# Attention scores of two heads at once on the two row halves of the matrix array, three products for a pair of heads

## The chip, the cores and the metric

The kernel runs on one core of a Trainium2 chip. The metric is the device time of one execution in microseconds (us). The kernel before took 719.02 us (median of 3 runs, 718.4 to 719.49). The engines are TensorE (PE; its weight loads are listed apart as PEld), VectorE (DVE), ScalarE (ACT), GpSimd (POOL) and SyncE (SP), which issues nearly all DMAs.

## What is computed

One decoder block over 512 tokens and 1024 channels, in float32: a retention branch (4 heads) and a forgetting-attention branch (8 heads of 64 channels), merged by sigmoid gates, followed by a SwiGLU feed-forward network. The change lies in the attention branch, which the reference computes for each head and each block of 128 queries as follows (cut):

```python
q_f = rmsnorm(q_f.reshape(B, S, FOX_HEADS, FOX_DH), g_fox_q[l])     # 8 heads of 64
k_f = rmsnorm(k_f.reshape(B, S, FOX_HEADS, FOX_DH), g_fox_k[l])
...
s = jnp.einsum('bhqd,bhkd->bhqk', q_blk, kh).astype(jnp.float32) * scale
s = s + c_blk[..., None] - c[:, :, None, :]          # cumulative forget-gate bias
s = jnp.where(mask[None, None], s, -jnp.inf)
p = jax.nn.softmax(s, axis=-1)
return jnp.einsum('bhqk,bhkd->bhqd', p.astype(vh.dtype), vh)
```

## The kernel before

Large products run in a one-pass float32 format (`float32r`). To keep float32 accuracy each operand is split into a high part h and a low part l = x - h, and a product is made of three: h*h, h*l and l*h (`three`, L165). ACT makes the high part with a cast, DVE the low part with a subtraction.

The work goes in stages: the input projections, the retention branch, the attention branch, the output projections and merge (`feat`, L529, with `w_y`), the output product `w_o`, and the feed-forward network. While a branch with long chains of small steps runs, PE is given other work between its pieces: the object `fill` (L554) holds generators of projection products, and `fill(us)` emits about so many microseconds of them. In the attention branch the fill is the tail of the value projection and the gate products `gates(0)` and `gates(1)` (products named acc<-xh,wh, acc<-xl,wh and acc<-xh,wl in the trace). PE's instructions in this branch are pinned to the order in which the code emits them (L553 to L644). Instructions emitted after L644 are not pinned: the scheduler may set the output projections of `w_y` (acc<-orh, acc<-orl, acc<-ofh, acc<-ofl) earlier, where it expects PE to wait.

The attention branch takes the 8 heads as 4 pairs a of heads e = 0, 1. The channels of a pair fill 128 rows, 64 for each head.

- `fox_prep(a, part)` (L458) turns k (part 0) or q (part 1) of a pair with four PE transposes into a PSUM bank of the tag `tp` and splits it. For each head it makes tiles of all 128 rows. `tk[e]` holds the high part of k twice, once on either half (two ACT passes, L467 and L468); `kl[e]` holds the low part on the head's own rows (DVE, L469) and zeros on the others, which POOL set once (L623). `tq[e]` holds the high part of q on the head's own rows (ACT, L477) and its low part on the other half (DVE, L478).
- `fox_scores(a, e, i)` (L481) makes the scores of one head and one query block i against keys 0 to n = 128(i+1): two products of 128 rows into a `sc` bank. The first (sc<-tk,tq) gives qh*kh + ql*kh, the second (sc<-kl,tq) gives qh*kl. The moving width is m = max(n, 256): 512, 384, 256 and 256 for i = 3, 2, 1, 0. POOL adds the causal mask to the bias (L491), DVE adds the bias and takes the row minimum (L499), ACT takes the exponential (L501), DVE the reciprocal and the scaling (L502, L503).
- `fox_turn(a, e, i)` (L506) turns the finished probabilities with i+1 PE transposes (tp<-ctab,pr) into a `tp` bank, and DVE (i = 3, L516) or ACT (L518) copies them to `pT`.
- `fox_values(a)` (L520) multiplies them with v for both heads (sc<-pT,vf; each head on one half of the array's columns) into a `sc` bank, which ACT and DVE split (L171, L172).

There are two `tp` and two `sc` banks. The loop at L629 walks the 32 head-blocks in the order i = 3, 2, 1, 0 within a head: at each step the scores of one head-block, the turn of the head-block three steps earlier (LAG = 3), after eight of them the values of a pair, and a piece of fill (SF, L133). The preparation of the next pair stands at steps 3 and 5 of 8.

In the retention branch, earlier in the kernel, four sets of products already use half of the array's rows: `ret_scores` (tp<-rT, L358) and the second part of `ret_values` (sc<-sn,rT, L385) have 64 rows, with even heads on the lower and odd heads on the upper half.

Of the kernel before, what the change touches and what calls it, by code (L numbers as in the profile page):

```python
# [21 lines left out]
NK = D // P  # L22
RH, RDK, RDV = 4, 64, 128
FH, FD = 8, 64
# [29 lines left out]
def block_kernel(ctx: ExitStack, tc, x, xT, c_early, c_tab, c_late, w_qf, w_tok, w_a, w_y, w_o, w_gu, w_dn, w_dh, out):  # L54
    nc = tc.nc
    PS = bass.MemoryType.PSUM
    tt, ts, stt = nc.vector.tensor_tensor, nc.vector.tensor_scalar, nc.vector.scalar_tensor_tensor
    act = nc.scalar.activation
# [12 lines left out]
    def mm(o, **kw):  # L71
        in_order(nc.tensor.matmul(o, **kw))  # L72

    def turn(o, src):
        in_order(nc.tensor.transpose(out=o, in_=src, identity=ident))  # L75

    def f32(ap):
        return ap.bitcast(F32)
# [7 lines left out]
    sm = ctx.enter_context(tc.tile_pool(name="sm", bufs=2, side="right"))  # L86
# [4 lines left out]
    def bank(tag):  # L91
        return ps.tile([P, 512], F32, name=tag, tag=tag, bufs={"acc": 4, "sc": 2, "tp": 2}[tag])
# [5 lines left out]
    gq = cst.tile([P, 1], F32, name="gq")  # L98
# [104 lines left out]
    for k in range(NK):  # L203
        h, l = first_units[k // 2]
# [111 lines left out]
    gp = nc.gpsimd  # L316
# [138 lines left out]
    ra, rb = slice(0, FD), slice(FD, P)  # L455
    fox = {}

    def fox_prep(a, part):  # L458

        if part == 0:  # L460
            tk = [fwk.tile([P, S], F32R, name="tk", tag=f"tk{e}", bufs=TB) for e in range(2)]
            kl = kls[a % TB]
            pk = bank("tp")
            for t in range(NT):
                turn(pk[:, t * P:(t + 1) * P], kf[:, t, a * P:(a + 1) * P])
            for e, (r, o) in enumerate(((ra, rb), (rb, ra))):
                act(out=tk[e][r], in_=pk[r], func=AF.Copy, scale=gk[r])  # L467
                act(out=tk[e][o], in_=pk[r], func=AF.Copy, scale=gk[r])  # L468
                stt(out=kl[e][r], in0=pk[r], scalar=gk[r], in1=f32(tk[e])[r], op0=ALU.mult, op1=ALU.subtract)  # L469
            fox["k", a] = tk, kl  # L470
        else:
            tq = [fwk.tile([P, S], F32R, name="tq", tag=f"tq{e}", bufs=TB) for e in range(2)]
            pq = bank("tp")
            for t in range(NT):
                turn(pq[:, t * P:(t + 1) * P], qf[:, t, a * P:(a + 1) * P])
            for e, (r, o) in enumerate(((ra, rb), (rb, ra))):
                act(out=tq[e][r], in_=pq[r], func=AF.Copy, scale=gq[r])  # L477
                stt(out=tq[e][o], in0=pq[r], scalar=gq[r], in1=f32(tq[e])[r], op0=ALU.mult, op1=ALU.subtract)  # L478
            fox["q", a] = tq

    def fox_scores(a, e, i):  # L481

        tq, (tk, kl) = fox["q", a], fox["k", a]
        if i == NT - 1:
            fox["cb"] = fox_bias(2 * a + e)
            fox["pT", a, e] = fwk.tile([P, 3 * 384 + S], F32, name="pT", tag="pT", bufs=PT)
        cb = fox["cb"]
        n = (i + 1) * P
        m = max(n, 256)
        qs = slice(i * P, n)  # L490
        gp.tensor_tensor(out=cb[:, qs], in0=cb[:, qs], in1=mask, op=ALU.add)  # L491
# [3 lines left out]
        pr = fwk.tile([P, S], F32, name="pr", tag="pr", bufs=PR)  # L495
        nm = sm.tile([P, 1], F32, name="nm", tag="nm", bufs=4)
        rs = sm.tile([P, 1], F32, name="rs", tag="rs", bufs=4)
        ri = sm.tile([P, 1], F32, name="ri", tag="ri", bufs=4)
        nc.vector.tensor_tensor_reduce(out=pr[:, :n], in0=cb[:, :n], in1=sc[:, :n], scale=-1.0, scalar=3e38,  # L499
                                       op0=ALU.add, op1=ALU.min, accum_out=nm)  # L500
        fox["last"] = act(out=pr[:, :n], in_=pr[:, :n], func=AF.Exp, scale=-1.0, bias=nm, accum_out=rs)  # L501
        nc.vector.reciprocal(out=ri, in_=rs)  # L502
        ts(out=pr[:, :n], in0=pr[:, :n], scalar1=ri, scalar2=None, op0=ALU.mult)  # L503
        fox["pr", a, e, i] = pr

    def fox_turn(a, e, i):  # L506

        pr, pT = fox["pr", a, e, i], fox["pT", a, e]
        pt = bank("tp")
        for j in range(i + 1):  # L510
            turn(pt[:, j * P:(j + 1) * P], pr[:, j * P:(j + 1) * P])
        row = pT[:, i * P:(i + 1) * P]
        dst = bass.AP(tensor=row.tensor, offset=row.offset, ap=[row.ap[0], [384, i + 1], [1, P]])
        src = pt[:, :(i + 1) * P].rearrange("p (j q) -> p j q", j=i + 1)
        if i == 3:
            nc.vector.tensor_copy(out=dst, in_=src)  # L516
        else:
            nc.scalar.copy(out=dst, in_=src)  # L518
# [98 lines left out]
    ofl = ofp.tile([P, 4, S], F32R, name="ofl")  # L617

    fill(CF[2])
    kls = [[fwk.tile([P, S], F32R, name="kl", tag=f"kl{b}{e}", bufs=1) for e in range(2)] for b in range(TB)]  # L620
    for pair in kls:
        for e, o in enumerate((rb, ra)):
            gp.memset(f32(pair[e])[o], 0.0)  # L623
    fox_prep(0, 1)
    fill(CF[3])
    fox_prep(0, 0)
    fill(PF)
    chain = [(a, e, i) for a in range(4) for e in range(2) for i in reversed(range(NT))]
    for s in range(len(chain) + LAG + 2):  # L629
        if s < len(chain):  # L630
            fox_scores(*chain[s])
            if s % 8 in PREP and s // 8 < 3:
                fill(SF[0] / 2)
                fox_prep(s // 8 + 1, PREP.index(s % 8))
        if LAG <= s < len(chain) + LAG:
            fox_turn(*chain[s - LAG])
        v = s - LAG - 1
        if v >= 0 and v % 8 == 7:
            if v == 7:
                fill.until(2)  # L640
            fox_values(v // 8)
        fill(SF[chain[min(s, len(chain) - 1)][2]])
    fill.until(1)
    pinned[0] = False  # L644
    fwk.release()
# [417 lines left out]
```

## Time and profile before

| | before |
|---|---|
| median of 3 runs (range) | 719.02 us (718.4 to 719.49) |
| profiled execution: time | 720.08 us |
| profiled execution: span of the profile | 718.3 us |
| clock granted to TensorE | 1.00 |
| PE busy | 708.7 us, 99% of the span |
| PEld busy | 623.2 us, 87% |
| DVE busy | 508.9 us, 71% |
| ACT busy | 343.8 us, 48% |
| POOL busy | 70.7 us, 10% |

A matmul row of the timeline gives its start and a modelled duration. Matmuls overlap, so the pace is read from the distance between starts: a product of width 512 lasts 0.39 us by its row, but the next starts about 0.23 us later. For the same reason PE's busy share is high even where it waits a little; a wait shows as a distance between starts that is larger than the pace. One float32 product (not float32r) appears as two records, so four products are x8. The median of the shown runs lies 1.06 us below the profiled execution.

### The profile page before, as it was taken

The numbers are of one execution on the slowest core, as the hardware profiler recorded it, in microseconds if no ns is written. First come the engines' busy times: TensorE is split into PE (matmuls) and PEld (weight loads), VectorE is DVE, ScalarE is ACT, GpSimd is POOL, SyncE is SP. The second block draws the span as 40 slices with busy tenths as digits, with TensorE's granted clock in tenths as the row PEclk, the third lists the DMA queues.
The fourth block names the chain that finished last, engine by engine and source line by source line (L and its number), as shares of the span: only waits on it lengthen the run. The fifth ranks groups of instructions, "written<-read, shape, count | busy, mean of one in ns | idle before, by whom it ended". The sixth has DMA issues, their size and how long they took to land.

```text
span 718.3 us, 10861 instructions
## 1 busy us (share of the span) xinstructions
PE 708.7 (99%) x4307; PEld 623.2 (87%) x4307; DVE 508.9 (71%) x844; ACT 343.8 (48%) x532; POOL 70.7 (10%) x90
## 2 busy tenths in 40 slices
PE   8999999999999999999999999999999999999997
PEld 6888998888776688888888999999999997888997
DVE  6343667756878664536968889898989998834694
ACT  4532334446666733324653755565565545422241
POOL 0163502212221100000120000000000000000000
PEclk9999999999999999999999999999999999999999
DMA  8632222234212033237403323332233124631111
GB/s 278 253 118 89 74 76 74 75 107 149 99 45 74 29 103 103 88 91 256 180 1 117 112 69 114 118 118 70 109 118 118 59 67 131 205 127 59 57 63 60
DMA packets 19908, 76.34 MB, mean 106 GB/s; under 512 B 2312, under 2 KB 2952, under 8 KB 16656
## 3 DMA queue, kind: packets, MB, share of 16 engines
q1 hardware_dynamic: 19712, 75.62, 31.0%
q8 instruction: 34, 0.56, 0.3%
q14 instruction: 18, 0.15, 0.1%
q10 hardware_dynamic: 144, 0.02, 0.0%
HBM read 73.52 MB, written 2.11 MB: 105 GB/s over the span
## 4 chain that ended last, share of the span: by engine, by line
PE 92%; DVE 3%; ACT 2%; DMA 2%; issue 1%; POOL 0%; SPq 0%; DVEq 0%; ACTq 0%
PE acc L72 60%; PE sc L72 26%; PE tp L72 5%; PE tp L75 2%; DMA t<-in_w_dn_dram 1%; DVE pr L499 1%; DMA raw<-in_w_tok_dram 1%; POOL cb L491 0%; ACT ah L862 0%; DVE pr L503 0%; ACT xfh L692 0%; DVE tq L478 0%; ACT pr L501 0%; DVE kl L469 0%; ACT tk L468 0%
## 5 line engine op out<-in xcount | busy, mean ns | idle before, releaser
L152 ACT CAST wh<-raw 128x1024 fp32r<-128x1024 f32 (+1 forms) x52 | 54.5, 1050 | 122.5 <-PE acc L72 97.4
L153 DVE TENSOR_TENSOR wl<-raw,wh 128x1024 fp32r<-128x1024 f32 (+1 forms) x52 | 66.6, 1282 | 47.6 <-ACT wh L152 47.4
L72 PE MATMUL sc<-xfh,cl 128*128 128x256 f32 x288 | 83.3, 289 | 0.0
L72 PE MATMUL sc<-xfh,ch 128*128 128x256 f32 x288 | 81.6, 283 | 1.2 <-DVE u L944 1.0
L72 PE MATMUL sc<-xfl,ch 128*128 128x256 f32 x288 | 81.4, 283 | 0.0
L72 PE MATMUL acc<-wh,xh 128*128 128x512 f32 (+2 forms) x192 | 69.7, 363 | 0.1
L740 DVE TENSOR_TENSOR cl<-t,ch 128x1024 fp32r<-128x1024 f32 x48 | 58.6, 1222 | 13.7 <-ACT ch L740 13.6
L72 PE MATMUL acc<-wh,xl 128*128 128x512 f32 (+2 forms) x192 | 68.2, 355 | 0.0
L72 PE MATMUL acc<-wl,xh 128*128 128x512 f32 (+2 forms) x192 | 68.0, 354 | 0.0
L72 PE MATMUL acc<-xfh,ah 128*128 128x256 f32 (+1 forms) x216 | 63.9, 296 | 0.0
L72 PE MATMUL acc<-xfh,al 128*128 128x256 f32 (+1 forms) x216 | 63.7, 295 | 0.0
L72 PE MATMUL acc<-xfl,ah 128*128 128x256 f32 (+1 forms) x216 | 63.7, 295 | 0.0
L740 ACT CAST ch<-t 128x1024 fp32r<-128x1024 f32 x48 | 50.5, 1053 | 12.8 <-PE tp L72 8.0
L72 PEld LDWEIGHTS sc<-xfh,ch 128*128 128x128 f32 x288 | 55.1, 191 | 1.6 <-issue 1.2
L72 PEld LDWEIGHTS sc<-xfh,cl 128*128 128x128 f32 x288 | 55.0, 191 | 0.9 <-DVE cl L740 0.2
L72 PEld LDWEIGHTS sc<-xfl,ch 128*128 128x128 f32 x288 | 55.1, 191 | 0.0
L72 PE MATMUL acc<-xh,wh 128*128 128x512 f32 x128 | 51.8, 405 | 0.0
L72 PE MATMUL acc<-xh,wl 128*128 128x512 f32 x128 | 50.1, 391 | 0.0
L72 PE MATMUL acc<-xl,wh 128*128 128x512 f32 x128 | 49.9, 390 | 0.0
L740 DVE TENSOR_TENSOR al<-raw,ah 128x1536 fp32r<-128x1536 f32 x24 | 42.2, 1757 | 6.9 <-ACT ah L740 6.9
L72 PEld LDWEIGHTS acc<-xfh,al 128*128 128x128 f32 x216 | 41.3, 191 | 1.0
L72 PEld LDWEIGHTS acc<-xfl,ah 128*128 128x128 f32 x216 | 41.3, 191 | 0.9
(298 smaller groups left out, 1795.3 us busy)
## 6 DMA issues: line engine op xcount, KB each, us to landing
raw<-in_w_gu_dram SPq DMA_DIRECT2D x21, 1024.0 KB, 4.8
raw<-in_w_tok_dram SPq DMA_DIRECT2D x16, 512.0 KB, 3.6
raw<-in_w_a_dram SPq DMA_DIRECT2D x16, 512.0 KB, 3.6
t<-in_w_dn_dram SPq DMA_DIRECT2D x14, 512.0 KB, 3.7
raw<-in_w_y_dram SPq DMA_DIRECT2D x8, 512.0 KB, 3.7
raw<-in_w_o_dram SPq DMA_DIRECT2D x8, 512.0 KB, 3.7
raw<-in_w_dh_dram SPq DMA_DIRECT2D x4, 1024.0 KB, 6.4
xf<-in_xT_dram SPq DMA_DIRECT2D x8, 256.0 KB, 5.0
```

The costliest lines, as they stand in the source:

```text
L72: in_order(nc.tensor.matmul(o, **kw))
L75: in_order(nc.tensor.transpose(out=o, in_=src, identity=ident))
L152: nc.scalar.copy(out=h[:, :width], in_=raw[:, :width])
L153: tt(out=l[:, :width], in0=raw[:, :width], in1=f32(h)[:, :width], op=ALU.subtract)
L499: nc.vector.tensor_tensor_reduce(out=pr[:, :n], in0=cb[:, :n], in1=sc[:, :n], scale=-1.0, scalar=3e38, op0=ALU.add, op1=ALU.min, accum_out=nm)
L740: split_to.last = nc.scalar.copy(out=h, in_=src), tt(out=l, in0=src, in1=f32(h), op=ALU.subtract)
```

## The change

- `fox_prep` makes, for a pair, one high tile (`kh` or `qh`, one ACT pass over 128 rows) and one low tile (`kl` or `ql`, one DVE pass). The doubled and zero-padded halves are gone, and so are POOL's four memsets.
- `fox_scores(a, i)` makes both heads' scores of a query block: three products for each head (qh*kh, ql*kh, qh*kl), each on the 64 rows of its head, the heads alternating, each head into its own `sc` bank. The widths m stay. The softmax steps follow for e = 0, then e = 1.
- `fox_turn(a, i)` turns both heads' probabilities.
- The loop walks 16 pair-blocks. At step p it emits the values of the previous pair (at p % 4 == 2, followed by fill), then the turn of the pair-block two steps earlier, then the scores of block p, then fill with other amounts. The preparation of the next pair stands at p % 4 = 1 (k) and 2 (q).
- Buffers: `pT` 2 instead of 3, `pr` 6 instead of 4, bias rows `cb` 5 instead of 3. The fill ahead of the first scores is 4.0 instead of 5.9 us.

```diff
-    RAW, WB, SG, PT, PR, TB, CBUF = 2, 3, 8, 3, 4, 2, 3
-    PREP = [3, 5]
-    RF, CF, PF, SF, LAG = (5.32, 4.64, 5.6, 4.6, 11.2), (3.0, 2.0, 2.26, 4.0), 5.9, (0.83, 1.03, 1.77, 1.6), 3
+    RAW, WB, SG, PT, PR, TB, CBUF = 2, 3, 8, 2, 6, 2, 5
+    RF, CF, PF, SF = (5.32, 4.64, 5.6, 4.6, 11.2), (3.0, 2.0, 2.26, 4.0), 4.0, (3.6, 2.9, 1.0, 2.4)
...
-            for e, (r, o) in enumerate(((ra, rb), (rb, ra))):
-                act(out=tk[e][r], in_=pk[r], func=AF.Copy, scale=gk[r])
-                act(out=tk[e][o], in_=pk[r], func=AF.Copy, scale=gk[r])
-                stt(out=kl[e][r], in0=pk[r], scalar=gk[r], in1=f32(tk[e])[r], op0=ALU.mult, op1=ALU.subtract)
...
+        h = fwk.tile([P, S], F32R, name=nm + "h", tag=nm + "h", bufs=TB)
+        l = fwk.tile([P, S], F32R, name=nm + "l", tag=nm + "l", bufs=TB)
+        pk = bank("tp")
+        for t in range(NT):
+            turn(pk[:, t * P:(t + 1) * P], src[:, t, a * P:(a + 1) * P])
+        act(out=h, in_=pk, func=AF.Copy, scale=gain)
+        stt(out=l, in0=pk, scalar=gain, in1=f32(h), op0=ALU.mult, op1=ALU.subtract)
...
-        sc = bank("sc")
-        mm(sc[:, :m], lhsT=tq[e][:, qs], rhs=tk[e][:, :m], start=True, stop=False)
-        mm(sc[:, :m], lhsT=tq[e][:, qs], rhs=kl[e][:, :m], start=False, stop=True)
+        sc = [bank("sc") for _ in range(2)]
+        for g, (x, y) in enumerate(((qh, kh), (ql, kh), (qh, kl))):
+            for e, r in enumerate(heads):
+                mm(sc[e][:, :m], lhsT=x[r, qs], rhs=y[r, :m], start=g == 0, stop=g == 2)
...
-    chain = [(a, e, i) for a in range(4) for e in range(2) for i in reversed(range(NT))]
-    for s in range(len(chain) + LAG + 2):
-        if s < len(chain):
-            fox_scores(*chain[s])
-            if s % 8 in PREP and s // 8 < 3:
-                fill(SF[0] / 2)
-                fox_prep(s // 8 + 1, PREP.index(s % 8))
-        if LAG <= s < len(chain) + LAG:
-            fox_turn(*chain[s - LAG])
...
+    chain = [(a, i) for a in range(4) for i in reversed(range(NT))]
+    for p in range(len(chain) + 3):
+        if p >= 6 and p % 4 == 2:
+            if p == 6:
+                fill.until(2)
+            fox_values(p // 4 - 1)
+            fill(SF[2])
+        if 2 <= p < len(chain) + 2:
+            fox_turn(*chain[p - 2])
+        if p < len(chain):
+            fox_scores(*chain[p])
+            if p // 4 < 3 and p % 4 in (1, 2):
+                fill(SF[p % 4] / 2)
+                fox_prep(p // 4 + 1, p % 4 - 1)
+                fill(SF[p % 4] / 2)
+                continue
+        fill(SF[p % 4])
```

PE's first 755 rows and everything from the first `w_y` products behind the branch on are the same in both programs. In the middle of the branch, on PE before, the end of a head: scores (sc), a turn of probabilities (tp<-ctab,pr) and gate products (acc) take turns one head at a time.

```order
L72 MATMUL sc<-tk,tq 128x256
L72 MATMUL sc<-kl,tq 128x256
L75 MATMUL tp<-ctab,pr 128x128
L72 MATMUL acc<-xh,wh 128x512
L72 MATMUL acc<-xl,wh 128x512
L72 MATMUL acc<-xh,wl 128x512
L72 MATMUL sc<-tk,tq 128x256
L72 MATMUL sc<-kl,tq 128x256
```

The same place on PE in the changed kernel, here with what each row waits for; tp<-ctab,qf is the transposition of the next pair's q.

```order
L75 MATMUL tp<-ctab,qf 128x128 [waits DVE_49]
L75 MATMUL tp<-ctab,qf 128x128 x3
L72 MATMUL acc<-xh,wh 128x512
L72 MATMUL acc<-xl,wh 128x512
L72 MATMUL acc<-xh,wl 128x512
L75 MATMUL tp<-ctab,pr 128x128 [waits Activation_49]
L75 MATMUL tp<-ctab,pr 128x128 x2
L75 MATMUL tp<-ctab,pr 128x128 [waits Activation_49]
L75 MATMUL tp<-ctab,pr 128x128 x2
L72 MATMUL sc<-kh,qh 128x256 [waits DVE_49] x2
L72 MATMUL sc<-kh,ql 128x256 x2
L72 MATMUL sc<-kl,qh 128x256 x2
```

The scores of a pair-block now stand as one block of six products on half rows between full-row work, and the turns of both heads follow one another; the second head's turn waits for ACT. Towards the end of the branch, on PE before, the last head's scores stand with single `w_y` products between them.

```order
L72 MATMUL sc<-tk,tq 128x384
L72 MATMUL sc<-kl,tq 128x384
L75 MATMUL tp<-ctab,pr 128x128 x2
L72 MATMUL sc<-tk,tq 128x256
L72 MATMUL sc<-kl,tq 128x256
L75 MATMUL tp<-ctab,pr 128x128
L72 MATMUL acc<-ofh,wh 128x512
L72 MATMUL sc<-tk,tq 128x256
L72 MATMUL sc<-kl,tq 128x256
```

And in the changed kernel, the last pair's block i = 1:

```order
L75 MATMUL tp<-ctab,pr 128x128 x8
L72 MATMUL sc<-kh,qh 128x256
L72 MATMUL acc<-orh,wh 128x512
L72 MATMUL acc<-orl,wh 128x512
L72 MATMUL acc<-orh,wl 128x512
L72 MATMUL acc<-orh,wh 128x512
L72 MATMUL acc<-orl,wh 128x512
L72 MATMUL sc<-kh,qh 128x256
L72 MATMUL sc<-kh,ql 128x256 x2
L72 MATMUL sc<-kl,qh 128x256 x2
```

Here the scheduler has put full-row products between the first head's and the second head's first product, so that the block is entered twice. This happens three times, at the last pair's blocks i = 2, 1 and 0.

More of the change, by code (lines that the diff above doesn't have):

```diff
@@ L490, in fox_scores @@
         qs = slice(i * P, n)
-        gp.tensor_tensor(out=cb[:, qs], in0=cb[:, qs], in1=mask, op=ALU.add)
-        sc = bank("sc")
-        mm(sc[:, :m], lhsT=tq[e][:, qs], rhs=tk[e][:, :m], start=True, stop=False)
-        mm(sc[:, :m], lhsT=tq[e][:, qs], rhs=kl[e][:, :m], start=False, stop=True)
[L495 to L518, printed above, removed]
+        sc = [bank("sc") for _ in range(2)]
@@ new lines, in fox_turn @@
+    def fox_turn(a, i):
+        for e in range(2):
+            pr, pT = fox["pr", a, e, i], fox["pT", a, e]
+            pt = bank("tp")
+            for j in range(i + 1):
+                turn(pt[:, j * P:(j + 1) * P], pr[:, j * P:(j + 1) * P])
+            row = pT[:, i * P:(i + 1) * P]
+            dst = bass.AP(tensor=row.tensor, offset=row.offset, ap=[row.ap[0], [384, i + 1], [1, P]])
+            src = pt[:, :(i + 1) * P].rearrange("p (j q) -> p j q", j=i + 1)
+            if i == 3 and e == 0:
+                nc.vector.tensor_copy(out=dst, in_=src)
+            else:
+                nc.scalar.copy(out=dst, in_=src)
@@ L619, in block_kernel @@
     fill(CF[2])
[L620 to L623, printed above, removed]
     fox_prep(0, 1)
```

49 lines of the change are left out of this document (22 added, 27 removed).

## The prediction

> **What bounds the kernel now.** I read the page first, for the engine that carries the span and for the chain of work that ended last.
>
> ```profile
> span 718.3 us, 10861 instructions
> PE 708.7 (99%) x4307; PEld 623.2 (87%) x4307; DVE 508.9 (71%) x844; ACT 343.8 (48%) x532; POOL 70.7 (10%) x90
> PE 92%; DVE 3%; ACT 2%; DMA 2%; issue 1%; POOL 0%; SPq 0%; DVEq 0%; ACTq 0%
> ```
>
> PE is busy for 99% of the span and makes 92% of the chain. The attention branch gives PE gate products between its steps, so PE is the bound there too: what the change is worth is PE's time for the rows that differ, and PE's waits among them. The table of stretches for the part of PE's order that differs (84.0 us) shows the other engines:
>
> ```profile
> core 0: us, PE busy (x) PEld busy (x) DVE busy (x) ACT busy (x) POOL busy (x), PEclk, DMA share, GB/s
> 166.10:250.10 84.00, 82.42 (x440) 63.10 (x439) 62.87 (x171) 57.11 (x130) 17.22 (x30) 1.00 0.22 71
> ```
>
> DVE is busy for 75% and ACT for 68%, so neither bounds the stretch as a whole; but PE waits for single steps of theirs. The granted clock is 1.00 and DMA stands at 0.22, so I keep both out of the sum. From PE's timeline I take the pace of the scores, as distances between starts:
>
> ```profile
> 168.79 0.39 PE L72 MATMUL sc<-tk,tq 128*128 128x512 f32 x1
> 169.01 0.39 PE L72 MATMUL sc<-kl,tq 128*128 128x512 f32 x1
> 169.24 0.39 PE L72 MATMUL acc<-xh,wh 128*128 128x512 f32 x1
> ...
> 171.28 0.33 PE L72 MATMUL sc<-tk,tq 128*128 128x384 f32 x1
> 171.45 0.34 PE L72 MATMUL sc<-kl,tq 128*128 128x384 f32 x1
> 171.63 0.40 PE L72 MATMUL acc<-xh,wh 128*128 128x512 f32 x1
> ...
> 173.01 0.28 PE L72 MATMUL sc<-tk,tq 128*128 128x256 f32 x1
> 173.12 0.28 PE L72 MATMUL sc<-kl,tq 128*128 128x256 f32 x1
> 173.24 0.40 PE L72 MATMUL acc<-xh,wh 128*128 128x512 f32 x1
> ```
>
> Two products take 0.45 us at width 512, 0.35 at 384 and 0.23 at 256: 0.225, 0.175 and 0.115 each, with nothing lost on entering or leaving, since all these rows use the whole array. PE's waits in the stretch show as larger distances:
>
> ```profile
> 206.93 0.40 PE L72 MATMUL acc<-orh,wh 128*128 128x512 f32 x1
> 207.57 0.50 PE L72 MATMUL sc<-tk,tq 128*128 128x512 f32 x1 [0.24 <-DVE nm L499]
> ...
> 224.51 0.40 PE L72 MATMUL acc<-orh,wh 128*128 128x512 f32 x1
> 225.48 0.33 PE L75 MATMUL tp<-ctab,pr 128*128 128x128 f32 x1 [0.57 <-ACT pT L518]
> ...
> 231.85 0.40 PE L72 MATMUL acc<-orh,wl 128*128 128x512 f32 x1
> 232.42 0.63 PE L75 MATMUL tp<-ctab,pr 128*128 128x128 f32 x4 [0.17 <-DVE pr L503]
> ...
> 240.81 0.40 PE L72 MATMUL acc<-ofh,wh 128*128 128x512 f32 x1
> 241.56 0.52 PE L75 MATMUL tp<-ctab,pr 128*128 128x128 f32 x3 [0.34 <-DVE pr L503]
> ```
>
> Against the pace of 0.23 the four lose 0.41, 0.74, 0.34 and 0.52, together 2.0 us. The smaller ones, each under 0.4, I estimate at 1.4 more: 3.4 us of waits.
>
> **Part one, the products.** Before, a query block of a pair costs two heads times two products, four widths in line. After, it is three for each head, and if the two heads' products run at the same time, three widths. The pair's four blocks have one product each at 0.225 and 0.175 and two at 0.115, 0.63 us for one product of each block; four pairs save 4 x 0.63 = 2.5 us. Whether halves run at the same time is seen in the retention branch, where products of 64 rows stand beside full-row ones (float32, each x8 is four products of width 128):
>
> ```profile
> 95.56 1.05 PE L72 MATMUL sc<-vr,sT 128*128 128x128 f32 x8
> 96.54 0.72 PE L72 MATMUL sc<-sn,rT 64*128 64x128 f32 x8
> 97.09 0.71 PE L72 MATMUL tp<-rT 64*128 64x128 f32 x8
> ...
> 134.66 1.05 PE L72 MATMUL sc<-vr,sT 128*128 128x128 f32 x8
> 135.64 0.72 PE L72 MATMUL sc<-sn,rT 64*128 64x128 f32 x8
> 136.29 0.50 PE L72 MATMUL acc<-wh,xh 128*128 128x512 f32 x1
> 136.63 0.40 PE L72 MATMUL acc<-wl,xh 128*128 128x512 f32 x1
> ```
>
> Eight full-row records take 0.98 us, eight half-row ones 0.55: on the two halves they do overlap. No row shows it for float32r, so the bounds are three widths (-2.5 us) and six, one after the other: 4 x 0.63 x 2 = +5.0 us. I take the first, since the nearest row is the same array at the same row split.
>
> A rule of the Trainium skill gives less here: "TensorE: Matmul & The Clock Gate", Part 3, "Measured speedup vs the span model", reports 3.07 for four row tiles, 77% of the full factor. As an estimate, 1.53 instead of 2 would make the three widths cost 3.9 and leave 0.2 us of the 2.5, so that the forecast would lie 2.3 us higher. The retention rows speak for nearly the full factor once entering and leaving are taken out.
>
> **Part two, entering and leaving.** The same rows give the price. Leaving: half rows before half rows take 0.55 (96.54 to 97.09), the same work before full rows 0.65 (135.64 to 136.29), so the change of mode costs 0.10 at the border. Then 0.98 for eight full-row records holds one such border and leaves 0.88, 0.11 each. In the 0.55 four steps of two at once, 0.44, leave 0.11: the first weights after the border are not loaded ahead. The same shows behind the block, where the next gate product starts 0.34 later (136.29 to 136.63) instead of 0.23. In and out therefore cost 0.10 + 0.11 + 0.10 + 0.11 = 0.42, and I use 0.4 for rounding. Sixteen pair-blocks give 16 x 0.4 = +6.4 us. The lower bound is 0.2 a block, +3.2, if the weights of float32r can be loaded ahead; the upper 0.5, +8.0. I take 6.4, as the row that follows here is the same kind of gate product. Before, none of this was paid for the scores.
>
> In the changed order the last pair's blocks i = 2, 1 and 0 have `w_y` products between the two heads' first products. Each then enters and leaves twice (0.4) and has one width that runs alone (0.175, 0.115 and 0.115): 1.6 us if nothing covers it. The filler stands there because the second `sc` bank is expected late, so part falls into waits that would be there anyway: +0.8, between 0 and 1.6.
>
> The Trainium skill, "TensorE: Matmul & The Clock Gate", Part 3, "The mechanism", lets a weight load overlap a running product only where the row groups differ; by that rule the alternating heads would be better off than full rows. The case's weight loads on the whole array speak against it:
>
> ```profile
> 168.56 0.19 PEld L72 LDWEIGHTS sc<-tk,tq 128*128 128x128 f32 x1
> 168.79 0.19 PEld L72 LDWEIGHTS sc<-kl,tq 128*128 128x128 f32 x1
> ```
>
> The load for kl,tq starts with the product tk,tq and is hidden beneath it. By the rule the 64 old products would each pay 0.19 us, and the new ones nothing: 12 us of gain that the pace of 0.225 leaves no room for.
>
> **Part three, ACT and DVE.** The groups of ACT and DVE in the branch (count, busy us, mean ns, idle before):
>
> ```profile
> L468 ACT ACTIVATE tk<-tp,ce 64x512 fp32r<-64x512 f32 x8 | 5.5, 683 | 0.1
> L477 ACT ACTIVATE tq<-tp,gq 64x512 fp32r<-64x512 f32 x8 | 5.4, 681 | 1.7 <-DVE tq L478 1.2 <-PE tp L75 0.2
> L467 ACT ACTIVATE tk<-tp,ce 64x512 fp32r<-64x512 f32 x8 | 5.4, 679 | 2.5 <-DVE kl L469 2.4
> L478 DVE SCALAR_TENSOR_TENSOR tq<-tp,gq,tq 64x512 fp32r<-64x512 f32 x8 | 6.0, 750 | 1.0 <-ACT tq L477 0.8
> L469 DVE SCALAR_TENSOR_TENSOR kl<-tp,ce,tk 64x512 fp32r<-64x512 f32 x8 | 6.0, 750 | 6.1 <-ACT tk L468 6.1
> L499 DVE CUSTOM_DVE_ANT_0 pr<-cb,sc 128x256 f32<-128x256 f32 x8 | 3.3, 414 | 0.4 <-POOL cb L491 0.4
> L501 ACT ACTIVATION_READ_ACCUMULATOR pr<-pr,nm 128x1 f32 x32 | 6.0, 187 | 0.0
> L501 ACT ACTIVATE pr<-pr,nm 128x256 f32<-128x256 f32 x8 | 4.1, 511 | 5.7 <-DVE nm L499 5.3 <-DVE ri L502 0.4
> L518 ACT COPY pT<-tp 128x384 f32<-128x384 f32 x8 | 3.8, 470 | 1.3 <-PE tp L75 1.2
> ```
>
> ACT makes 24 passes of 0.68 us and will make 8, with the same 512 elements in a row: 16 x 0.68 = 11 us less. DVE makes 16 passes and will make 8: 8 x 0.75 = 6 us less. None of it is on PE, so it counts only through waits. The softmax steps, turns and values keep their number and widths. POOL's memsets and the order of SP's bias loads lie beside PE's work; in the open they would cost a bias load's landing, for which I add nothing as the first four are issued together ahead of the scores.
>
> New waits come from two places. The turn of a pair needs two `tp` banks; beside the preparation of q, the second head's turn waits for ACT. From the end of a block's scores (width 256) a row minimum (0.41), two exponentials with the reading of their sums (0.51 + 0.19 each), the cast of q (0.68) and the copy of the first head's turn (0.47) stand in line, 3.0 us; PE has six gate products (6 x 0.23) and seven transposes (0.11 each, the float32 record of part two) until it needs that bank, 2.2 us. That is 0.8 us at two places in the middle, 1.6 in all. And each block needs both `sc` banks, so the values' bank must be split before the scores of the next block. In the old kernel scores need one bank at a time. On the other side, the lighter ACT and DVE should take away most of the 2.0 us quoted above. I put the waits of the new kernel at 2.7 us, between 0 and 6: -0.7 against 3.4.
>
> **The sum.** -2.5 + 6.4 + 0.8 - 0.7 = +4.0 us. The profiled execution took 720.08, so its like would take 724.1; the median of the runs shown lies 1.06 lower, at 719.02, and the forecast is 723.0. A measurement of this kernel can tell about 0.2% from no change, 1.4 us.
>
> **The rivals.**
> - *Slower by more: float32r products do not overlap on the two halves.* Then part one is +5.0 instead of -2.5 and all else stays: +11.5, 730.5. For it: no row shows float32r on half rows. Against it: the float32 rows overlap. Chance 0.10.
> - *About the same: PE's waits go.* Two heads at once put more filler between a score and its turn, and ACT has 11 us less to do; if all 3.4 us of waits go and the split blocks cost nothing: -2.5 + 6.4 - 3.4 = +0.5, 719.5. For it, the waits quoted are for ACT's copies and DVE's scaling, whose queues get shorter; against it, the tail keeps its chain of softmax steps. Chance 0.20.
> - *Faster: the borders are half hidden.* If float32r weights are loaded ahead across the border, a block pays 0.2 instead of 0.4; with the waits gone too: -2.5 + 3.2 - 3.4 = -2.7, 716.3. With all waits gone, a block has to cost less than 0.28 for a gain over 1.4 us. For it: PE's loads run ahead elsewhere. Against it: 0.34 instead of 0.23 is a float32r product. Chance 0.17.
>
> **How the numbers follow.** The forecast, slower by 1.5 to 8 us, has 0.53; its own range is 720.5 to 727. The slower side is 0.53 + 0.10 and a little of the second case, 0.65; the second case leaves 0.18 for the same, and faster keeps 0.17. From 716.5 to 728 all is held but the first rival and the lower half of the third.
>
> **What would show it.** Right: the scores of a block as pairs of rows with starts almost together; a gap of about 0.2 us ahead of each block, and the first product behind it at 0.34; the stretch of 84.0 us growing to 88. Wrong in part one: six equal distances within a block. Wrong in part two: a first product behind a block at 0.23. Wrong in part three: waits over 6 us, or none, between the first scores and the last values; the row of the second head's turn beside tp<-ctab,qf shows it first.

## The result

The changed kernel takes 723.03 us (median of 6 runs, 721.98 to 724.3). The kernel before, run beside it, takes 718.77 (6 runs, 718.35 to 719.49). The ratio is 1.0060, 95% interval 1.0048 to 1.0072: 4.3 us slower, where 4.0 was forecast. That the total agrees proves little; the terms behind it are gone through below, and two of them were off.

The page of the changed kernel, its span, its engines and its chain:

```profile
span 720.9 us, 10889 instructions
PE 710.1 (99%) x4339; PEld 619.4 (86%) x4339; DVE 501.0 (70%) x832; ACT 334.7 (46%) x520; POOL 65.1 (9%) x86
PE 92%; DMA 2%; DVE 2%; ACT 1%; issue 1%; SPq 0%; DVEq 0%; ACTq 0%
```

ACT has lost 9 us of work and DVE 8 (11 and 6 were worked out). Most of that difference has a cause that the description of the change leaves out: at i = 3 DVE now copies only the first head's turn (`if i == 3 and e == 0`), and ACT the second's, so four copies of 0.6 to 0.7 us have moved from DVE to ACT. PE still makes 92% of the chain, with 32 products more than before. The stretch in which PE's order differs, from the same gate product on one side to the same row on the other (83.84 us before, by the starts of rows):

```profile
core 0: us, PE busy (x) PEld busy (x) DVE busy (x) ACT busy (x) POOL busy (x), PEclk, DMA share, GB/s
165.50:252.20 86.70, 85.03 (x471) 60.49 (x470) 57.99 (x164) 49.87 (x120) 12.48 (x28) 1.00 0.19 61
```

It is 2.9 us longer. PE's timeline of the first block of scores, to be held against the rows of 168.79 to 169.24 in the prediction:

```profile
165.52 0.39 PE L72 MATMUL acc<-xh,wl 128*128 128x512 f32 x1
165.84 0.50 PE L72 MATMUL sc<-kh,qh 64*128 64x512 f32 x2
166.17 0.40 PE L72 MATMUL sc<-kh,ql 64*128 64x512 f32 x2
166.41 0.40 PE L72 MATMUL sc<-kl,qh 64*128 64x512 f32 x2
166.73 0.50 PE L72 MATMUL acc<-xh,wh 128*128 128x512 f32 x1
167.07 0.40 PE L72 MATMUL acc<-xl,wh 128*128 128x512 f32 x1
167.31 0.39 PE L72 MATMUL acc<-xh,wl 128*128 128x512 f32 x1
```

Each x2 is one product of either head. The steps are 0.32, 0.33, 0.24, 0.32, 0.34, 0.24. The five steps from 165.52 to 167.07 take 1.55, where five at the pace of 0.227 would take 1.14. Four of them hold the border: 0.09 before the block, 0.10 behind its first products, 0.09 after the block and 0.11 behind the first gate product, 0.39 in all.

PE's waits are now at the turn of the second head beside the preparation of q, the place that the prediction named:

```profile
178.53 0.49 PE L75 MATMUL tp<-ctab,pr 128*128 128x128 f32 x3
180.05 0.55 PE L75 MATMUL tp<-ctab,pr 128*128 128x128 f32 x3 [1.04 <-ACT pT L511]
...
200.62 0.49 PE L75 MATMUL tp<-ctab,pr 128*128 128x128 f32 x3
201.68 0.55 PE L75 MATMUL tp<-ctab,pr 128*128 128x128 f32 x3 [0.57 <-ACT pT L511]
```

Three transposes take about 0.32; the distances are 1.52 and 1.06, so 1.2 and 0.7 us are waited. The block that is entered twice, i = 2 of the last pair:

```profile
229.72 0.39 PE L72 MATMUL acc<-orh,wh 128*128 128x512 f32 x1
230.17 0.44 PE L72 MATMUL sc<-kh,qh 64*128 64x384 f32 x1
230.54 0.50 PE L72 MATMUL acc<-orl,wh 128*128 128x512 f32 x1
...
231.20 0.44 PE L72 MATMUL sc<-kh,qh 64*128 64x384 f32 x1
231.21 0.61 PE L72 MATMUL sc<-kh,ql 64*128 64x384 f32 x2
```

The first head's first product stands alone between gate products and pays the border for itself.

**Two differences lie outside the stretch.** One belongs to the profiled execution of before. Its first products, then the same of the changed kernel:

```profile
5.76 0.76 PE L72 MATMUL sc<-wh,xh 128*128 128x512 f32 x1 [0.87 <-DVE wh L195]
...
7.09 1.05 PE L72 MATMUL tp<-wh,xh 128*128 128x512 f32 x2
7.95 1.05 PE L72 MATMUL sc<-wh,xl 128*128 128x512 f32 x2
```

```profile
5.68 0.47 PE L72 MATMUL sc<-wh,xh 128*128 128x512 f32 x1 [0.90 <-DVE wh L194]
...
6.41 0.62 PE L72 MATMUL tp<-wh,xh 128*128 128x512 f32 x2
6.86 0.62 PE L72 MATMUL sc<-wh,xl 128*128 128x512 f32 x2
```

Two products take 0.86 us in the one (7.09 to 7.95) and 0.45 in the other (6.41 to 6.86), steps of 0.43 against 0.23: until 9.6 us the profiled execution of before ran at half pace. The last gate product that both programs share ahead of the stretch starts at 166.52 there and at 165.52 in the changed kernel. That 1.0 us is the start of this execution, not the change. The profiled spans differ by 2.6 us and the medians by 4.3; this start accounts for 1.0 of the 1.7 between them, and another 0.4 lies outside the span of the profile, where the changed kernel's execution has 2.2 us and the other 1.8.

The other lies at 596 us, in the feed-forward network, 345 us behind the last changed instruction. PE's waits there before, and in the changed kernel:

```profile
PE sc L72 <- ACT d L808: 1.5, 1, 1.5
```

```profile
PE sc L72 <- ACT d L799: 2.4, 1, 2.4
```

PE waits for a copy on ACT, and ACT's queue stands behind a cast that waits for a weight transfer. That cast, before and after:

```profile
594.77 1.05 ACT L862 CAST ah<-t 128x1024 fp32r<-128x1024 f32 x1 [1.71 <-DMA t<-in_w_dn_dram]
```

```profile
597.32 1.05 ACT L853 CAST ah<-t 128x1024 fp32r<-128x1024 f32 x1 [2.57 <-DMA t<-in_w_dn_dram]
```

The same transfer costs 0.9 us more. This was not foreseen; experiments 9 to 11 show why.

### The profile page after: what moved, and what is told of

Read it like the earlier page. It is cut to its first block, busy times and chain, and to the rows that moved or that the text cites. A ratio compares the mean times of both kernels' runs of the same rounds, so it can differ in the third digit from the quotient of the medians.

```text
span 720.9 us, 10889 instructions
## 1 busy us (share of the span) xinstructions
PE 710.1 (99%) x4339; PEld 619.4 (86%) x4339; DVE 501.0 (70%) x832; ACT 334.7 (46%) x520; POOL 65.1 (9%) x86
## 4 chain that ended last, share of the span: by engine, by line
PE 92%; DMA 2%; DVE 2%; ACT 1%; issue 1%; SPq 0%; DVEq 0%; ACTq 0%
PE acc L72 61%; PE sc L72 25%; PE tp L72 4%; PE tp L75 2%; DMA raw<-in_w_tok_dram 1%; DMA t<-in_w_dn_dram 1%; DVE cl L731 0%; ACT xfh L683 0%; DVE al L854 0%; DVE ot L922 0%; ACT qf L439 0%; ACT ah L853 0%; DVE t L740 0%; DVE pf L896 0%; DVE pr L491 0%
```

## The experiments

Theory: both heads run at the same time, which gives the 2.5 us; each entry into half rows costs 0.39 us, which takes 6.2 us for sixteen and 7.4 for nineteen; the rest is waits. Rivals: the halves do not really overlap; or the loop over pairs with its waits makes the time, whatever the rows. Each ratio is against runs of the kernel before that were taken beside the experiment; a gap is the distance between two starts, and half pace means steps of 0.43 us between products of width 512 instead of 0.23. Where the text says "in the branch", it compares the time in the traces between two products that all the kernels share, one ahead of the attention branch and one behind it (at 138.23 and 259.65 us before).

**1. Head after head.**

```
-        for g, (x, y) in enumerate(((qh, kh), (ql, kh), (qh, kl))):
-            for e, r in enumerate(heads):
+        for e, r in enumerate(heads):
+            for g, (x, y) in enumerate(((qh, kh), (ql, kh), (qh, kl))):
```

> The changed kernel with one head's three products before the other's, so that only the last of the first head and the first of the second can run together. Theory (the halves overlap): five widths in line instead of three, 2 x 0.63 us for each of four pairs, +5.0; its program enters half rows 17 times instead of 19, about -0.8; so 727 us against 723.0. Rival (float32r products on the two halves do not overlap anyway): 723, no difference, and equal distances between the six starts of a block.

725.0 us (5 runs), ratio 1.0085 (1.0072 to 1.0098). The experiment did not do what it was for. In the program all three products of the first head now stand ahead of the second's, but in fourteen of the sixteen blocks they start in pairs on the chip as before:

```profile
165.43 0.50 PE L72 MATMUL sc<-kh,qh 64*128 64x512 f32 x2
165.76 0.40 PE L72 MATMUL sc<-kh,ql 64*128 64x512 f32 x2
166.00 0.40 PE L72 MATMUL sc<-kl,qh 64*128 64x512 f32 x2
```

Only in the last pair's blocks i = 2 and i = 1 does the second head come later, and there the heads run in line:

```profile
230.29 0.44 PE L72 MATMUL sc<-kh,qh 64*128 64x384 f32 x1
230.57 0.33 PE L72 MATMUL sc<-kh,ql 64*128 64x384 f32 x1
230.75 0.33 PE L72 MATMUL sc<-kl,qh 64*128 64x384 f32 x1
230.90 0.44 PE L72 MATMUL sc<-kh,qh 64*128 64x384 f32 x1
```

So the order of the heads is of no account where the second one has not to wait. Of the 2 us on top of the changed kernel 0.6 lie in the branch; the rest has another source (below, at 596 us). To force all products into line took another edit.

**2. Both heads on the same half.** The second head's scores are left out and the first's are made twice, so that all six products use the same 64 rows.

```
-                mm(sc[e][:, :m], lhsT=x[r, qs], rhs=y[r, :m], start=g == 0, stop=g == 2)
+                mm(sc[e][:, :m], lhsT=x[heads[0], qs], rhs=y[heads[0], :m], start=g == 0, stop=g == 2)
```

> The changed kernel with the second head of a pair computed from the first head's rows of q and k, so that both heads' products use the same half of the array's rows (the second head's scores are left out, the first's are computed twice). Number, shape and order of all instructions stay. Theory (the two halves run at the same time, which saves three widths a block; the loss is the border of 0.39 us a block and the waits): six widths in line instead of three, 4 x 0.63 x 3 = 7.5 us more than the changed kernel's 723.0, so 730.5. Rival (the halves overlap only in the records, and the time of the changed kernel is that of six products in line): no difference, 723.

730.95 us (4 runs), ratio 1.0161 (1.0148 to 1.0174).

```profile
166.18 0.73 PE L72 MATMUL sc<-kh,qh 64*128 64x512 f32 x2
166.75 0.63 PE L72 MATMUL sc<-kh,ql 64*128 64x512 f32 x2
167.22 0.62 PE L72 MATMUL sc<-kl,qh 64*128 64x512 f32 x2
167.77 0.50 PE L72 MATMUL acc<-xh,wh 128*128 128x512 f32 x1
```

Each pair now takes 0.47 to 0.57 instead of 0.24 to 0.33, and the whole costs 7.9 us by the medians, 7.3 by the ratios, against 7.5 worked out. Not all of that is scores: in the profiled execution (731.9) 6.6 us lie in the branch, with 0.3 less of waits, and 1.9 behind it, from 596 us on. The rows of the scores by themselves grow from 11.8 to 19.1 us, 7.3. The overlap is real and nearly full; the first rival of the prediction is out.

**3. Twelve entries more.** Behind the first pair of products a piece of fill is put, and its time taken off the next fill: 31 entries instead of 19, the same work.

```
                 mm(sc[e][:, :m], lhsT=x[r, qs], rhs=y[r, :m], start=g == 0, stop=g == 2)
+            if g == 0:
+                fill.step()
+                fill.debt -= S * MM3
```

> The changed kernel with three gate products (taken from the fill that follows) set between the first two and the last four products of each block, as long as there is fill: half rows are entered 31 times instead of 19, with the same work. Theory (0.4 us for each entering and leaving): 12 x 0.4 = +4.8, 727.8 us. Rival (the time of the change comes from the loop over pairs and its waits, not from the borders): within 0.5 us of 723.0.

730.76 us (5 runs, 729.45 to 732.92), ratio 1.0159 (1.0140 to 1.0178): 7.7 us for 4.8 expected. Of the rest, waits in the stretch grew from 1.9 to 3.0 us and the gap at 596 us from 2.75 to 3.34; behind it thirteen products ran at half pace (2.9 us) in the profiled execution, which took 732.38. The two executions with a granted clock of 1.000 took 729.45 and 729.65: 4.7 + 1.1 + 0.6 = 6.4 on 723.0. In the branch it takes 5.9 us more; less the 1.1 of waits that is 4.8, or 0.40 an entry. The price per entry holds, and the rival (within 0.5 us) is out; the experiment moved more than it meant to.

**4. Five entries less.** The last two query blocks of a pair, both of width 256, are made in one bank, back to back: 14 entries.

```
-        sc = [bank("sc") for _ in range(2)]
...
+        if i:
+            fox["sc"] = [bank("sc") for _ in range(2)]
+            for b in (1, 0) if i == 1 else (i,):
+                w = slice(256, 512) if b == 0 else slice(0, m)
...
+        sc = [b[:, 256:512] if i == 0 else b for b in fox["sc"]]
```

> The changed kernel with the scores of a pair's blocks i = 1 and i = 0 made together, both in one bank, so that half rows are entered 14 times instead of 19. Theory: -5 x 0.4 and about -0.2 for widths that no longer run alone: 720.8 us. Rival (waits for the banks make the time): 723 or more, since a bank is held longer.

723.34 us (5 runs), ratio 1.0055 (1.0041 to 1.0068): no gain; by its time, the rival's. The scores' rows do shrink, from 11.8 to 10.8 us. But waits in the stretch are 2.5 us, and the gap at 596 us is 3.32. In the branch the kernel does gain 1.6 us, or 2.1 with waits as before, 0.4 for each of five entries; the part behind the branch takes 0.7 of it back in the profiled execution.

**5. Pairs with full rows.** The loop over pairs and its buffers (bias rows 4 instead of 5) with the old preparation for each head and the old two full-row products.

```
...
+        for e in range(2):
+            mm(sc[e][:, :m], lhsT=tq[e][:, qs], rhs=tk[e][:, :m], start=True, stop=False)
+            mm(sc[e][:, :m], lhsT=tq[e][:, qs], rhs=kl[e][:, :m], start=False, stop=True)
...
```

> The loop over pairs, its fill and its buffers as in the changed kernel (bias rows 4 instead of 5, for room), but q and k prepared as before and two products on full rows for each head. Theory: +2.5 for the fourth width, -16 x 0.4 for the borders and -1.6 for the three blocks entered twice, +0 to +1 for the heavier preparation: 717.5 to 718.5 us, slightly under the kernel before. Rival (the loop over pairs makes the time): 723 or more.

722.11 us (5 runs), ratio 1.0036 (1.0023 to 1.0049): slower than before without any half rows. My theory missed it.

```profile
178.93 0.49 PE L75 MATMUL tp<-ctab,pr 128*128 128x128 f32 x3
181.37 0.55 PE L75 MATMUL tp<-ctab,pr 128*128 128x128 f32 x3 [1.95 <-ACT pT L512]
...
183.12 0.63 PE L72 MATMUL acc<-xh,wh 128*128 128x512 f32 x1
183.55 0.63 PE L72 MATMUL acc<-xl,wh 128*128 128x512 f32 x1
183.97 0.63 PE L72 MATMUL acc<-xh,wl 128*128 128x512 f32 x1
```

The wait for the second head's bank is 2.1 us here, and behind it eight gate products step by 0.43 instead of 0.23, 1.6 us. So the rival has a part of the truth: the loop over pairs is slow by itself, in the place where the preparation of q meets the two turns. The next two runs take that place away.

**6 and 7. The preparation one step earlier**, in the changed kernel and in the kernel of experiment 5.

```
-            if p // 4 < 3 and p % 4 in (1, 2):
+            if p // 4 < 3 and p % 4 in (0, 1):
...
-                fox_prep(p // 4 + 1, p % 4 - 1)
+                fox_prep(p // 4 + 1, p % 4)
```

> The changed kernel with the next pair's k prepared after a pair's first scores and q after its second, instead of after the second and the third. Number and shape of all instructions stay. Theory (PE waits for the second head's tp bank because ACT has the cast of q to do between the exponentials and the copy of the first head's turn; 1.2 + 0.7 us in the changed kernel): these two waits go, 723.0 - 1.9 = 721.1. Rival (ACT is late there whatever it does before, or the wait moves to the step that now has the cast beside it): no difference, 723.0.

724.2 us (6 runs, 722.07 to 725.35), ratio 1.0060 (1.0044 to 1.0076): no gain. Yet both waits are gone. The turn that waited 1.2 us now runs through, and from the first score to the last value the kernel takes 78.95 us (one gate product less lies in it) instead of 81.05, the 1.9 us that were expected:

```profile
178.92 0.82 PE L75 MATMUL tp<-ctab,pr 128*128 128x128 f32 x6
```

They are given back at 596 us:

```profile
595.88 0.39 PE L72 MATMUL sc<-hl,al 128*128 128x512 f32 x1
599.25 1.22 PE L72 MATMUL sc<-hl,ah 128*128 128x512 f32 x2 [2.98 <-ACT d L799]
600.27 0.63 PE L72 MATMUL sc<-hl,al 128*128 128x512 f32 x1
600.70 1.05 PE L72 MATMUL acc<-hl,ah 128*128 128x512 f32 x2
```

A gap of 3.37 us, and then twelve products at 0.43 instead of 0.23; with the steps on either side of them that is 2.7 us. By the time, the rival's "no difference" was right; but the wait has not moved to a step beside the cast, as it had it, and the one at 596 us is another (experiments 9 to 11).

> The kernel with pairs but the old full-row products (722.1 us, with waits of 5.1 us in the stretch and products at half pace for 3.4 us behind the longest of them), with k and q of the next pair prepared one step earlier as well. Theory (the pair's loop is slow only through the waits beside the preparation of k and q and the slow pace behind them; half rows cost the rest): 1.2 + 2.1 + 0.7 us of waits and 1.7 us of slow pace go, 722.1 - 5.7 = 716.4, faster than both kernels. Rival (two heads at once need two tp banks at once, and the wait only moves): 721 to 723.

717.88 us (11 runs, 716.13 to 718.84), ratio 0.9977 (0.9968 to 0.9986), where 716.4 was expected: 1.6 us faster than before, the only kernel here that beats both. The full-row loop over pairs keeps 2.6 us of waits, of which this is the largest, but no half pace, and the gap at 596 us is 1.73.

```profile
PE tp L75 <- DVE pT L510: 1.0, 1, 1.0
```

**8. No block entered twice.** A block's first product also waits for DVE's last reading of the `sc` banks (`fox["free"]`), so that both are free: 16 entries.

```
+                first = nc.tensor.matmul(sc[e][:, :m], lhsT=x[r, qs], rhs=y[r, :m], start=g == 0, stop=g == 2)
...
+                if g == e == 0 and "free" in fox:
+                    tc.add_manual_dep(first.ins, fox["free"].ins.name, mybir.DependencyInfo(mybir.DependencyClass.Sync, mybir.DependencyReason.DATA), reason="both banks")
...
```

> The changed kernel with the first product of a block's scores waiting until both sc banks are free, so that no other product stands between the heads' first products and half rows are entered 16 times instead of 19. Theory (each of the three double entries costs a border of 0.39 us and a width of 0.12 to 0.18 alone, and hides no wait): 723.0 - 1.6 = 721.4. Rival (the filler between them covers a wait for the second bank that now shows): 723.0.

724.39 us (6 runs, 721.69 to 727.2), ratio 1.0070 (1.0048 to 1.0091). Inconclusive by its time, since the profiled execution again has a gap of 3.24 us at 596 and thirteen products at half pace; the two executions with a granted clock of 1.000 took 721.69 and 722.95. By its rows the scores shrink by 1.0 us and a wait of 0.6 appears ahead of the values at 233.9; in the branch the kernel gains 1.0. So 0.6 of the 1.6 us of the double entries was covered.

**9 to 11. Code against weights.** The gap at 596 us was 1.7 to 1.9 in the kernels with full rows (before, 5, 7) and 2.75 to 3.4 in all seven with half rows. The page lists two queues of instruction loads; the larger, q8, has 34 packets, 0.56 MB, 16 KB each. PE makes 4339 products and as many weight loads, so if these are PE's, one packet is 128 products of its code. The queue's packet nearest to the place, in windows of half a microsecond: before, it ran at 600.0 us; after, at 595.0, in the middle of the transfer that ACT waits for:

```profile
q8 instruction: 1, 0.02, 11.7%
```

In all seven half-row kernels (after, 1 to 4, 6, 8) it ran 2.3 to 3.8 us ahead of the late cast; in the three with full rows it came 5 us behind it. The change adds 32 products, a quarter of a packet's worth and 7.3 us at the pace of 0.227, and so moves every later load of PE's code ahead: against the late cast by 7.5 us, from 5.2 behind it before to 2.3 ahead of it after. The awaited transfer itself takes 4.6 to 5.2 us from issue to landing in the seven kernels, and 3.6 to 3.7 in the three. To test it without touching the attention, 36 products of the first projection are made as two of width 256, in three kernels: the kernel before, the kernel of experiment 6, and that kernel with the edit of experiment 4.

```
+            halves = [(slice(c, c + 256), slice(k % 2 * 512 + c, k % 2 * 512 + c + 256)) for c in (0, 256)] if k < 5 else [(slice(0, 512), cs)]
             for t in range(NT):
-                three(accs[t], xh[:, k, tqs[t]], xl[:, k, tqs[t]], h[:, cs], l[:, cs], False, k == NK - 1)
+                for o, c in halves:
+                    three(accs[t][:, o], xh[:, k, tqs[t]], xl[:, k, tqs[t]], h[:, c], l[:, c], False, k == NK - 1)
```

> The kernel before, with 36 products of the first projection (contraction tiles 2, 3 and 4) made as two of width 256 each: 36 more products on TensorE by the time the attention starts, and the same work; two of 0.120 us for one of 0.227 cost 36 x 0.013 = 0.5 us. Theory (TensorE's code is loaded in pieces of 16 KB, one each 128 products; the 32 products that the change adds bring one such load into the time of the weight transfer that TensorE waits for at 596 us, so the wait grows from 1.5 to 2.3 to 2.9 us in every kernel with half rows, and products at half pace may follow): the same happens here without any half rows, the load comes at 592 to 594 us and the wait is 2.3 us or more: 719.2 + 0.5 + 0.8 to 1.4 = 720.5 to 721.1, more if products at half pace follow. Rival (the longer wait belongs to the half rows or to the order of the transfers): wait 1.5 us, 719.7.

722.95 us (6 runs, 720.23 to 724.34), ratio 1.0051 (1.0037 to 1.0064). The code load now runs at 591.5 us, and PE's waits and ACT's cast become:

```profile
PE sc L72 <- ACT d L810: 2.2, 1, 2.2
```

```profile
594.90 1.05 ACT L864 CAST ah<-t 128x1024 fp32r<-128x1024 f32 x1 [2.43 <-DMA t<-in_w_dn_dram]
```

The wait grew from 1.5 to 2.2 (2.3 or more was expected) in a kernel with no half rows, as the theory has it and its rival not; the transfer takes 4.4 us instead of 3.7; the profiled execution (720.23) shows no half pace. The other five show granted clocks of 0.994 to 0.998 and took 722.2 to 724.3. The median is 3.8 us above before, 1.8 more than the top of what I expected without half pace. Products at half pace in those five would fit, but there is no trace of them.

> The changed kernel with the early preparation of k and q (724.2 us, with a wait of 2.9 us at 596 and ten products at half pace behind it), and with the same 36 products of the first projection split in two. Theory (code load against transfer): the load comes at about 590 us, ahead of the awaited transfer; the wait is back at about 1.5 us and the half pace (10 x 0.21 = 2.1 us) is gone: 724.2 + 0.5 - 1.4 - 2.1 = 721.2. Rival: nothing of it goes, 724.7.

720.97 us (11 runs, 720.02 to 722.18), ratio 1.0023 (1.0014 to 1.0031). The same edit that slows the kernel before brings this one from 1.0060 down. The code load runs at 588.0 us, ahead of the transfer, which takes 3.7 us again, and the wait is back:

```profile
PE sc L72 <- ACT d L801: 1.5, 1, 1.5
```

> The same as the kernel before it here, with the scores of the last two query blocks of a pair made together in one bank, so that half rows are entered 14 times instead of 19. Theory (each entry costs 0.39 us): 5 x 0.39 = 2.0 us less than the kernel beside it, 719.2 if that takes 721.2, so that half rows come level with the kernel before and no further. Rival (the price is in the waits, not in the entries): the same time as the kernel beside it.

718.90 us (12 runs, 717.84 to 720.39), ratio 0.9998 (0.9989 to 1.0008): level with before. Five entries are worth 720.97 - 718.90 = 2.07 us, 0.41 each (in the branch 1.7 us, with 0.4 more of waits). With the wait at 596 us out of the way, the price that experiment 4 could not show is there.

All kernels together. The columns branch and behind are differences to the kernel before in the profiled executions: in the branch, and from there to PE's last product. Waits are those over 0.3 us between the first score and the last value; half pace counts products in the profiled execution. The runs of before beside the experiments had medians of 718.77 to 719.69 us, so kernels are compared by the ratio.

| kernel | entries | branch, us | behind, us | waits, us | gap at 596, us | half pace | median, us | ratio |
|---|---|---|---|---|---|---|---|---|
| before | 0 | 0 | 0 | 2.4 | 1.89 | 0 | 718.77 | 1 |
| changed | 19 | +2.9 | +0.7 | 1.9 | 2.75 | 0 | 723.03 | 1.0060 |
| 1 head after head | 17 | +3.5 | +2.6 | 2.1 | 3.13 | 7 | 725.0 | 1.0085 |
| 2 same half | 19 | +9.5 | +2.6 | 1.6 | 3.22 | 7 | 730.95 | 1.0161 |
| 3 twelve entries more | 31 | +8.8 | +4.0 | 3.0 | 3.34 | 13 | 730.76 | 1.0159 |
| 4 five entries less | 14 | +1.2 | +1.4 | 2.5 | 3.32 | 0 | 723.34 | 1.0055 |
| 5 pairs, full rows | 0 | +2.6 | -0.1 | 4.8 | 1.79 | 8, at 183 | 722.11 | 1.0036 |
| 6 early preparation | 19 | +1.0 | +3.9 | 0 | 3.37 | 12 | 724.2 | 1.0060 |
| 7 full rows, early | 0 | -1.4 | -0.2 | 2.6 | 1.73 | 0 | 717.88 | 0.9977 |
| 8 whole blocks | 16 | +1.9 | +4.0 | 2.5 | 3.24 | 13 | 724.39 | 1.0070 |
| 9 before, split | 0 | 0 | +0.4 | 2.4 | 2.61 | 0 | 722.95 | 1.0051 |
| 10 early, split | 19 | +0.9 | -0.2 | 0 | 1.85 | 0 | 720.97 | 1.0023 |
| 11 early, split, five less | 14 | -0.8 | -0.2 | 0.4 | 1.81 | 0 | 718.90 | 0.9998 |

## Why the prediction was right

**Products, -2.5: right.** Three widths a block, halves together, by the rows and by experiment 2 (the scores' rows take 7.3 us more without the overlap, 7.5 worked out). The Trainium skill, "TensorE: Matmul & The Clock Gate", Part 3, "Measured speedup vs the span model", gives 3.07 for four row tiles. The lower factor for two halves that the prediction estimated from it, which would have left 0.2 us of the gain, is not seen here: the pairs step by 0.24.

**Borders, +6.4: right.** 0.39 a block by the rows, 6.2 us for sixteen; 0.40 an entry by experiment 3, and 0.41 between experiments 10 and 11. The retention rows of another number format and width gave the price to 0.03 us. The third rival (half hidden borders) is out.

**Double entries, +0.8: about right.** The rows show 0.39 and a width for each of three, some 1.6 us; by experiment 8 about 1.0 of it is in the open.

**Waits, -0.7: mis-sized, at both ends.** Before, I counted 3.4 us and missed one inside the last pair's values, where the second head's products start 0.7 us behind the first's. Before and after:

```profile
244.29 3.06 PE L72 MATMUL sc<-pT,vf 128*64 128x512 f32 x16
```

```profile
244.78 2.38 PE L72 MATMUL sc<-pT,vf 128*64 128x512 f32 x16
```

Sixteen products take 0.7 less where nothing is waited for, so 4.1 us stood there. After, there are the 1.9 at the two turns and some 0.3 of small ones, so the term is -1.9. The step that named the second head's turn beside the preparation of q was right in place and nearly in size (0.8 twice; 1.2 and 0.7), and most of the other 1.1 us did not come. The second rival needed all waits gone. The 2.7 was a guess within 0 to 6; experiment 5 shows how far it could have gone, 4.8 us with the same loop and the heavier preparation.

**A term that was not in the sum: +0.9.** The weight transfer at 596 us. All was taken to stay as it was in the 470 us behind the branch, because PE's order there is the same; but the order of instructions is not the time at which their code is loaded. Of the 0.9 us 0.7 are left at the end. That they make good most of the 1.2 us by which the waits came out lower is luck.

**The base.** The profiled execution lay 1.06 us above the median of before, and the half pace at its start cost 1.0. The two agree, but the other executions of before left no trace that would show their start. Taking the sum against its time and then subtracting that difference comes to the same as taking it against the median.

By the rows the terms make -2.5 + 6.2 + 1.6 - 1.9 = 3.4 in the stretch, where 2.9 is seen; the 0.5 between them is not assigned. The 2.9, the 0.7 behind the branch and the 0.4 outside the span are 4.0, within the 3.5 to 5.2 that the interval of the ratio leaves.

So the change loses because it buys 2.5 us of products with sixteen borders. Its lighter ACT and DVE do pay: with the same loop the waits are 1.9 us against 4.8 with the preparation for each head, and none against 2.6 once the preparation stands earlier. But in the earlier place the full-row products have the better of it all the same: a ratio of 0.9977 in experiment 7 against 0.9998 in experiment 11, which also has half a microsecond (an estimate) of split products in it. In the branch it is -1.4 us against -0.8.

## What to carry to other kernels

Half-row products are worth their time only in long runs: here an entry (0.39 us) costs as much as 1.7 products of width 512 (0.227), so a block of three widths that saves one loses, and blocks must be joined or the saving larger. When the loop of a pipelined branch is rebuilt, try the place of its preparation steps before judging the idea; the same edit was worth 4.2 us with full rows. And when an edit that removes a wait does not shorten the kernel, look for the time behind the branch, at the next place where PE waits for a transfer.

## What the runs showed of the hardware that was not expected

**Code loads compete with weights.** A 16 KB load of PE's code within a 512 KB weight transfer makes its last part land about 0.7 to 1.6 us late (3.6 to 3.7 us from issue to landing without it, 4.4 to 5.2 with it; ACT waits 1.7 us without it, 2.4, 2.6 and 3.2 with it). "Advanced Engine Details and Errata" of the Trainium skill, section "ISA Cache", gives lines of 16 KB, 256 instructions; the 34 loads for 8678 products and weight loads, 255 each, agree. The load takes 11.7% of half a microsecond of sixteen engines, 0.94 us of one. In experiment 1 the last seven packets of the transfer end one by one, 0.16 us apart, when all the others have landed; before, the last three do. That the load and the data meet on one of the sixteen DMA engines is therefore likely, but no run shows the engine.

**Half pace behind a wait.** Gaps of 3.1 to 3.4 us at 596 us were followed in five of six profiled executions by 7 to 13 products at 0.43 instead of 0.23 us, beginning 3.2 to 4.6 us after the gap's start; gaps of 2.75 and less there by none. In experiment 5 a gap of 2.2 us had it too, 3 us behind one of 1.3. The Trainium skill, "TensorE: Matmul & The Clock Gate", Part 1, "HAM oscillation — how this bites in real kernels", names idle gaps of more than about 3.4 us as the limit, with the clock at half behind them. These runs agree in the factor (0.43 against 0.23), but all their gaps lie below that limit, and the runs decide. The slow products cost 1.6 to 2.9 us on top of the gap.

**The heads' order is free.** The first products of both heads start together, and the pairs step by 0.33 and 0.24 us as in the changed kernel, even where two products of the first head stand between them in the program (experiment 1, fourteen of sixteen blocks).
